# Scans of a three-block kernel on one Trainium2 core: output products regrouped, level runs merged

## The chip, the cores and the metric

One core of one Trainium2 chip runs the whole program. The metric is device time in microseconds (us), the median of several executions. TensorE (PE in the profile) multiplies matrices, its weight loads are PEld; ScalarE is ACT, VectorE is DVE, GpSimd is POOL, and SyncE (SP) issues the DMAs.

## The reference

The input is a sequence of 1024 tokens, 1024 wide. A first block (a delta-rule scan, a convolution, attention to a memory) is followed by two layers of a second one. Each layer has a GLA branch (4 heads, 32 key and 64 value channels), a differential attention branch and an HGRN branch (4 heads, 64 and 64). What matters here is the two-directional gated scan of the GLA and HGRN branches; in the reference it is

```python
def step(state, inp):
    g_n, u_n = inp
    return g_n[..., None] * state + u_n, state
...
o_inter = jnp.einsum('bhntk,bhnkv->bhntv', q * jnp.exp(bcum).astype(q.dtype), s_prev)
return (o_intra + o_inter).reshape(b_, h_, l_, dv).astype(v.dtype)
...
o_f = chunked_gated_scan(q, k_f, v, lg_f)
o_b = flip(chunked_gated_scan(flip(q), flip(k_b), flip(v), flip(lg_b)))
return o_f + o_b
```

So an output of a chunk is a sum of three things: what the forward state of the chunks before gives, what the backward state of the chunks behind gives, and what the tokens of the chunk itself give. Behind it stand a normalisation per head and a gate.

## The kernel before

The kernel keeps channels on the 128 partitions and tokens in the free dimension. The scans of a layer run in `scans` as three scans, i = 0 (GLA, G = 2: four heads of 32 key channels, in two groups g of one head pair each), and i = 1 and 2 (HGRN, G = 1: one head pair of 64 key channels each). A pair has heads e = 0 and 1. Chunks have 64 tokens, n = 0 to 15; j counts pairs of chunks, and x says which chunk of the pair it is, n = 2j + x. `quads` gives the order of cells in which neighbours use different quarters of the array: (x, e) = (0,0), (1,1), (0,1), (1,0).

A scan has three parts. `scan_prep` loads gates and makes decays. `scan_levels` builds the products of tokens within a chunk (AT) over seven levels: for each level and each group, `pairs` makes 32 products of 64 x 64, KK by QQ, into two PSUM banks (`aps`), 16 for the first four j and 16 for the rest, and calls `burst` behind each half. ScalarE (level 0) or VectorE under a mask (levels 1 to 6) takes the two banks into AT. Two banks are all that the pool `a` has. The level's KK comes from a pool of three buffers (tag `kk`), in which the states `S` of both directions lie too. `scan_out` transposes the keys (`KT`), makes the chunk sums (`up`), scans them (`ust`, then `S`, held in `sb[0]` forward and `sb[1]` backward), and writes the output: for each group g and each half hb of the chunks one block into two banks (`ops`). Bank b takes what contracts over partitions HEADS[b]. A block begins with a product with the zero tile `zz` into each bank, which opens all 512 columns (start), and every other product adds. Cell by cell follow a forward state product, a backward state product, both into bank e, and a value product (Vst by AT) into bank x. Then ScalarE copies bank 0 into `os`, VectorE adds bank 1, a burst follows, and `finish_head` of the block before (`last`): Square on ScalarE (`fr<-os`), a product with ones (`fst`), Ln and Exp, then two VectorE operations and the store. There are four blocks a layer for i = 0 and two each for i = 1 and 2, sixteen in all.

A burst is 12 matmuls of 128x512 from a stream of dense projections (`ps`); one call in 14 (SKIP) does nothing. While `pinned` is set, TensorE runs in the order in which the program is written (`mm`, line 250, keeps it). ScalarE, VectorE and SP run in order too, but there a scheduler sets the order when the program is built.

Of the kernel before, what the change touches and what calls it, by code (L numbers as in the profile page):

```python
# [11 lines left out]
BF16 = mybir.dt.bfloat16  # L12
# [134 lines left out]
class Stream:  # L147
# [5 lines left out]
    def burst(self, n=1):  # L153
        while n and (self.g or self.q):
            if self.g is None:
                self.g = self.q.popleft()()
            if self.g is None or next(self.g, True):
                self.g = None
            else:
                n -= 1  # L160
# [18 lines left out]
class Kern:  # L179
# [1290 lines left out]
    def scans(self, l, stream):  # L1470
        nc, tc = self.nc, self.tc
        with ExitStack() as es:
            pool = lambda n, b, **kw: es.enter_context(self.tpool(name="s" + n, bufs=b, **kw))
            p1, p2 = self.s1, self.s2 = pool("1", 1), pool("2", 2)
            self.s3 = pool("3", 3)
            self.fl, self.qt, self.qa, self.qo = (pool("fl", 2, space=PSUM), pool("t", 2, space=PSUM),
                                                 pool("a", 2, space=PSUM), pool("o", 2, space=PSUM))
            self.msk = p1.tile([128, 384], U8, name="msk")
            m = self.staged()[:, 0:384]
            nc.sync.dma_start(out=m, in_=self.A["masks"])  # L1480
            nc.vector.tensor_copy(out=self.msk, in_=m)
            self.zz = p1.tile([1, 128], BF16, name="zz")
            nc.vector.memset(self.zz, 0.0)
            lb = self.lower_bounds(p1) if l else None
            count = iter(range(1000))

            def burst():
                if next(count) % SKIP:
                    stream.burst()
            self.rot = None  # L1490
            left = len(stream.q)
            self.value_rows(stream, l)
            nxt = self.scan_prep(0, l, lb)
            stream.feed(PV)
            self.pinned = True
            for i in range(3):
                cur = nxt
                self.scan_levels(cur, burst)
                if i == 0:
                    stream.reach(left)  # L1500
                if i < 2:
                    nxt = self.scan_prep(i + 1, l, lb)
                else:
                    stream.reach(NEED)
                    qk = self.diff_qk(0, l)
                self.scan_out(cur, l, self.V("hgrn_norm" if i else "gla_norm", l), burst)
            self.pinned = False
            self.head0 = qk, self.diff_v(0, l, self.qt, "t")
            stream.feed(1000)
# [107 lines left out]
    def scan_levels(self, I, burst):  # L1617
# [11 lines left out]
        def pairs(KK, QQ, li):  # L1629
            for g in range(G):  # L1630
                aps = [self.qa.tile([128, 512], F32, tag="a", name="aps") for _ in range(2)]
                for j0 in (0, 4):
                    for j, n, x, e in self.quads(j0, j0 + 4):
                        ns, r = slice(n * 64, n * 64 + 64), cells[2 * g + e][0]
                        self.mm(aps[e][HEADS[x], j * 64:j * 64 + 64], KK[r, ns], QQ[r, ns])
                    burst()
                for e in range(2):
                    dst = AT[g][:, e * 512:e * 512 + 512]
                    if li == 0:
                        self.act(dst, aps[e])  # L1640
                    else:
                        m = self.msk[:, 64 * (li - 1):64 * li].rearrange("p (o c) -> p o c", o=1).to_broadcast([128, 8, 64])
                        nc.vector.copy_predicated(out=c8(dst), mask=m, data=c8(aps[e]))

        KK = T("kk", self.s3)
        self.tt(KK, kf, kb, ALU.add)
# [30 lines left out]
    def scan_out(self, I, l, nw, burst):  # L1677
# [44 lines left out]
        for g in range(G):  # L1722
            for hb in range(2):
                ops = [self.qo.tile([128, 512], F32, tag="o", name="ops") for _ in range(2)]
                for t in ops:
                    self.mm(t, self.zz, self.const[0:1, 0:256].bitcast(BF16), True, False)
                for j, n, x, e in self.quads(4 * hb, 4 * hb + 4):
                    r, h = cells[2 * g + e][0], HEADS[x]
                    o = [t[HEADS[e], n % 8 * 64:n % 8 * 64 + 64] for t in ops]
                    ns, c = slice(n * 64, n * 64 + 64), 512 * e + 64 * j  # L1730
                    last_ = j % 4 == 3 and x != e
                    if n > 0:
                        self.mm(o[e], sb[0][r, n - 1], Q[0][r, ns], False, last_ and n == 15)
                    if n < 15:
                        self.mm(o[e], sb[1][r, 14 - n], Q[1][r, ns], False, last_)
                    self.mm(o[x], Vst[g][h, j, HEADS[e]], AT[g][h, c:c + 64], False, last_)
                o = p2.tile([128, 512], F32, tag="os", name="os")
                self.act(o, ops[0])
                self.tt(o, o, ops[1], ALU.add)
                burst()  # L1740
                last()
                sl = slice(hb * 512, hb * 512 + 512)
# [29 lines left out]
```

## Time and profile before

| | |
|---|---|
| median of 3 runs | 3976.39 us (3974.06 to 3981.07) |
| the profiled execution | 3974.71 us, its span 3972.9 us |
| TensorE busy | 3663.0 us, 92% of the span |
| VectorE, ScalarE, GpSimd busy | 2322.0, 1889.2, 821.7 us |
| mean granted TensorE clock | 0.957 |
| matmul records of the level products (`aps`) | 3584 |
| matmul records of the output products (`ops`) | 960 of states, 512 of values, 32 of zeros |

A float32 matmul leaves two records, one for each of its passes, so 960 records are 480 products. In a timeline a row is a run of equal records: its start, its length to the end of its last record, and how many there were. Records overlap, so the step from one start to the next is what a product costs. The granted clock is a share of 2.4 GHz; the profile knows two levels, 1.2 and 2.4 GHz.

### The profile page before, as it was taken

To read this page: it belongs to the slowest core of one execution; us is meant where nothing else is said; L and a number is where in the kernel's file an instruction comes from. 1 tells how busy PE (TensorE), PEld (TensorE's weight loads), DVE (VectorE), ACT (ScalarE), POOL (GpSimd) and SP (SyncE) were. 2 spreads that over 40 slices of the span, in tenths; PEclk is the share of its full clock that TensorE was granted. 3 is DMA by queue.
4 is the path that set the end of the run, shared out by engine and by line. 5 is a ranking of instruction groups with operands and counts; after the bars stand their busy time and mean duration, and the time that the engine had idled before them with its cause. 6 is when DMAs were issued, how large, how long until landed. Compare 5 with 4: busy or idle time off the path is not lost. (4 is left out here: it accounts for less than half of the span.)

```text
span 3972.9 us, 69665 instructions
## 1 busy us (share of the span) xinstructions
PE 3663.0 (92%) x27554; PEld 2847.4 (72%) x27554; DVE 2322.0 (58%) x4491; ACT 1889.2 (48%) x3429; POOL 821.7 (21%) x710
## 2 busy tenths in 40 slices
PE   7999999999898999989999999999789899998897
PEld 5877666766666677767788667777677667777686
DVE  4246677777767777555544634464883553555863
ACT  4334444444444454444433444454774453545862
POOL 1003323333323333340223200012112100022111
PEclk9999999999999999999999999799999998899998
DMA  4422222222222222347444442222202431223113
GB/s 149 142 88 69 79 79 80 74 77 78 84 79 76 77 85 86 105 154 237 157 154 136 152 141 78 72 84 97 74 33 97 144 111 63 84 94 104 56 35 110
DMA packets 222583, 394.62 MB, mean 99 GB/s; under 512 B 24624, under 2 KB 44080, under 8 KB 222128
## 3 DMA queue, kind: packets, MB, share of 16 engines
q1 hardware_dynamic: 222256, 390.17, 29.5%
q8 instruction: 216, 3.54, 0.4%
q14 instruction: 111, 0.91, 0.1%
HBM read 268.44 MB, written 121.63 MB: 98 GB/s over the span
## 5 line engine op out<-in xcount | busy, mean ns | idle before, releaser
L250 PE MATMUL ps<-hh,whi 128*128 128x512 f32 (+2 forms) x3056 | 1293.2, 423 | 27.6 <-DVE st L202 8.1
L250 PE MATMUL ps<-hl,whi 128*128 128x512 f32 (+2 forms) x3056 | 1207.6, 395 | 4.5 <-DVE hl L202 4.5
L250 PE MATMUL ps<-hh,wlo 128*128 128x512 f32 (+2 forms) x3056 | 1207.3, 396 | 4.7 <-DVE wlo L202 4.6
L250 PEld LDWEIGHTS ps<-hh,whi 128*128 128x128 f32 (+1 forms) x3056 | 585.6, 192 | 199.0 <-issue 31.4
L250 PEld LDWEIGHTS ps<-hh,wlo 128*128 128x128 f32 (+1 forms) x3056 | 585.8, 192 | 138.3 <-DVE wlo L202 6.2
L250 PEld LDWEIGHTS ps<-hl,whi 128*128 128x128 f32 (+1 forms) x3056 | 587.4, 192 | 132.1 <-issue 20.5
L199 ACT ACTIVATE whi<-wraw 128x512 fp32r<-128x512 f32 x486 | 302.6, 625 | 570.0 <-PE ps L250 439.5
L202 DVE TENSOR_TENSOR wlo<-wraw,whi 128x512 fp32r<-128x512 f32 x398 | 294.2, 742 | 417.6 <-ACT whi L199 383.8
L202 POOL TENSOR_TENSOR uacg<-uacg,ut 128x512 f32<-128x512 f32 x240 | 337.6, 1407 | 789.9 <-ACT ut L569 656.1
L202 POOL TENSOR_TENSOR st<-st,rope 128x512 f32<-128x512 f32 x64 | 91.3, 1447 | 978.0 <-DVE st L415 946.5
L199 ACT ACTIVATE st<-ps 128x512 f32<-128x512 f32 (+2 forms) x260 | 149.3, 575 | 264.5 <-PE ps L250 223.9
L573 DVE SCALAR_TENSOR_TENSOR uacc<-uh,vecs,uacc 128x512 f32<-128x512 f32 x224 | 208.3, 930 | 8.0 <-ACT uacc L565 7.1
L202 POOL TENSOR_TENSOR acc<-acc,sq 128x512 f32<-128x512 f32 (+1 forms) x91 | 125.0, 1381 | 294.7 <-ACT sq L199 293.2
L202 POOL TENSOR_TENSOR wlo<-wraw,whi 128x512 fp32r<-128x512 f32 x88 | 121.8, 1385 | 286.7 <-ACT whi L199 259.9
L1387 DVE TENSOR_REDUCE D<-sc 128x1 f32<-128x1024 f32 x128 | 154.7, 1219 | 34.5 <-PE sc L250 33.9
L569 ACT ACTIVATE ut<-uh,vecs 128x512 f32<-128x512 f32 x240 | 166.0, 715 | 4.4 <-POOL uacg L202 3.5
L199 ACT ACTIVATE p<-sc,D 128x1024 f32<-128x1024 f32 x128 | 142.8, 1116 | 41.1 <-DVE D L1387 39.1
L250 PE MATMUL o_ps<-h,wT 128*128 128x128 f32 x1024 | 137.2, 282 | 19.1 <-ACT wT L199 19.1
L250 PEld LDWEIGHTS o_ps<-h,wT 128*128 128x128 f32 x1024 | 131.1, 197 | 27.7 <-ACT wT L199 22.8
L250 PE MATMUL sc<-h,h 128*128 128x512 f32 x256 | 94.0, 448 | 40.7 <-ACT p L199 40.4
L1380 POOL CAST qz<-h 64x128 fp32r<-64x128 f32 x128 | 54.3, 424 | 313.3 <-PE sc L250 304.2
L250 PE MATMUL ps<-oh,wlo 128*128 128x512 f32 x256 | 103.1, 403 | 4.6 <-DVE wlo L202 4.6
(334 smaller groups left out, 6092.8 us busy)
## 6 DMA issues: line engine op xcount, KB each, us to landing
wraw<-in_w_in_dram SPq DMA_DIRECT2D x326, 256.0 KB, 2.8
wraw<-in_w_out_dram SPq DMA_DIRECT2D x76, 256.0 KB, 2.7
g<-st SPq DMA_DIRECT2D x48, 256.0 KB, 2.3
y<-st SPq DMA_DIRECT2D x48, 256.0 KB, 2.0
gt<-y SPq DMA_DIRECT2D x48, 256.0 KB, 2.9
wraw<-in_w_mem_kv_dram SPq DMA_DIRECT2D x32, 256.0 KB, 3.0
yp<-gt SPq DMA_DIRECT2D x32, 256.0 KB, 3.4
yt<-yp SPq DMA_DIRECT2D x32, 256.0 KB, 3.1
```

Source lines behind the costliest of these rows:

```text
L199: self.nc.scalar.activation(out=out, in_=in_, func=func, **kw)
L202: (eng or self.nc.vector).tensor_tensor(out=out, in0=a, in1=b, op=op)
L250: self.pin(self.nc.tensor.matmul(out, lhsT=lhsT, rhs=rhs, start=start, stop=stop))
L569: keep(nc.scalar.activation(out=t, in_=u[:, j:j + 512], func=AF.Copy, scale=w(j)))
L573: keep(nc.vector.scalar_tensor_tensor(out=acc, in0=u[:, k:k + 512], scalar=w(k), in1=acc, op0=ALU.mult, op1=ALU.add))
L1380: nc.gpsimd.tensor_copy(out=Qz[slot][c][HEADS[c]], in_=Qs[c][HEADS[c], ts_])
L1387: nc.vector.reduce_max(out=D[:, c:c + 1], in_=sc, axis=AX.X, negate=True)
```

## The change

The zero tile and its two products per block go. The products of a block are grouped: all forward state products, then all backward ones, then all value products. The first state product into each bank starts it, and the first value product into a bank's other half starts that half. Bank b holds states and values for head b and, in its other half, values alone; so the evacuation is one ScalarE copy of 64 rows per head, and an add of half the columns. In `pairs` the two halves become one run of 32 products, and the two bursts stand behind the evacuation.

```diff
-            self.zz = p1.tile([1, 128], BF16, name="zz")
-            nc.vector.memset(self.zz, 0.0)
...
-                for j0 in (0, 4):
-                    for j, n, x, e in self.quads(j0, j0 + 4):
-                        ns, r = slice(n * 64, n * 64 + 64), cells[2 * g + e][0]
-                        self.mm(aps[e][HEADS[x], j * 64:j * 64 + 64], KK[r, ns], QQ[r, ns])
-                    burst()
+                for j, n, x, e in self.quads():
+                    ns, r = slice(n * 64, n * 64 + 64), cells[2 * g + e][0]
+                    self.mm(aps[e][HEADS[x], j * 64:j * 64 + 64], KK[r, ns], QQ[r, ns])
                 for e in range(2):
...
+                for _ in range(2):
+                    burst()
...
-                for t in ops:
-                    self.mm(t, self.zz, self.const[0:1, 0:256].bitcast(BF16), True, False)
+                part = lambda b, e, n: ops[b][HEADS[e], n % 8 * 64:n % 8 * 64 + 64]
+
+
+                new = [True, True]
+                for d, n0 in ((0, -1), (1, 14)):
+                    for j, n, x, e in self.quads(4 * hb, 4 * hb + 4):
+                        r, sn = cells[2 * g + e][0], n0 - n if d else n + n0
+                        if 0 <= sn < 15:
+                            self.mm(part(e, e, n), sb[d][r, sn], Q[d][r, n * 64:n * 64 + 64], new[e], False)
+                            new[e] = False
                 for j, n, x, e in self.quads(4 * hb, 4 * hb + 4):
-                    r, h = cells[2 * g + e][0], HEADS[x]
-                    o = [t[HEADS[e], n % 8 * 64:n % 8 * 64 + 64] for t in ops]
-                    ns, c = slice(n * 64, n * 64 + 64), 512 * e + 64 * j
-                    last_ = j % 4 == 3 and x != e
-                    if n > 0:
-                        self.mm(o[e], sb[0][r, n - 1], Q[0][r, ns], False, last_ and n == 15)
-                    if n < 15:
-                        self.mm(o[e], sb[1][r, 14 - n], Q[1][r, ns], False, last_)
-                    self.mm(o[x], Vst[g][h, j, HEADS[e]], AT[g][h, c:c + 64], False, last_)
+                    h, c = HEADS[x], 512 * e + 64 * j
+                    self.mm(part(x, e, n), Vst[g][h, j, HEADS[e]], AT[g][h, c:c + 64], x != e and j % 4 == 0, j % 4 == 3)
                 o = p2.tile([128, 512], F32, tag="os", name="os")
-                self.act(o, ops[0])
-                self.tt(o, o, ops[1], ALU.add)
+                two = lambda t, e, x: t[HEADS[e]].rearrange("p (j x c) -> p j x c", x=2, c=64)[:, :, x]
+                for e in range(2):
+                    self.act(o[HEADS[e]], ops[e][HEADS[e]])
+                    self.tt(two(o, e, 1 - e), two(o, e, 1 - e), two(ops[1 - e], e, 1 - e), ALU.add)
                 burst()
```

On TensorE, at the first output block of the first layer's scan i = 0 (h are the decayed queries, S the states, AT the products within a chunk, Vst the values), before:

```order
L250 LDWEIGHTS zz
L250 MATMUL ops<-const,zz 128x512
L250 LDWEIGHTS zz
L250 MATMUL ops<-const,zz 128x512
L250 MATMUL ops<-h_22196,S 64x64
L250 MATMUL ops<-AT_22356,Vst 64x64
L250 MATMUL ops<-h_22194,S 64x64
L250 MATMUL ops<-h_22196,S 64x64
L250 MATMUL ops<-AT_22356,Vst 64x64
```

and now the whole block, to the first dense product behind it:

```order
L250 MATMUL ops<-h_22192,S 64x64 x14
L250 MATMUL ops<-h_22194,S 64x64 x16
L250 MATMUL ops<-AT_22354,Vst 64x64 x16
L250 MATMUL ps<-hh_94,whi 128x512
```

State and value products no longer alternate: 30 of the one form stand ahead of 16 of the other, the forward states' first.

On ScalarE, at the end of the same scan (kk are the copies for the next scan's levels and h of 128x256x2 its queries, e and h of 128x1024 the gates of the scan after that; st and whi belong to the dense stream, os and fr to the output), before:

```order
L199 ACTIVATE kk<-h_23403 128x512
L199 ACTIVATE kk<-h_23404 128x512
L199 ACTIVATE kk<-h_23403 128x256x2
L199 ACTIVATE os<-ops 128x512
L199 ACTIVATE kk<-h_23404 128x256x2
L199 ACTIVATE whi<-wraw 128x512
L199 ACTIVATE fr<-os 128x512
L199 ACTIVATE fr<-fst,const 128x512
```

and now, of the 25 rows from the first kk to the last block's fr<-os, the last twelve:

```order
L199 ACTIVATE whi<-wraw 128x512
L199 ACTIVATE st<-ps 128x512
L199 ACTIVATE h_24267<-h_23399 128x256x2
L199 ACTIVATE os<-ops 64x512
L199 ACTIVATE st<-st 128x512
L199 ACTIVATE h_24724<-h_24724 128x1024
L199 ACTIVATE st<-st,const 128x512
L199 ACTIVATE os<-ops 64x512
L199 ACTIVATE h_24720<-h_24720 128x1024
L199 ACTIVATE e<-h_24722 128x1024
L199 ACTIVATE st<-st 128x512
L199 ACTIVATE fr<-os 128x512
```

The last block's evacuation and Square moved behind the next levels' copies and behind half of the gates of the scan after it.

## Rows read from the trace of the kernel before

**Rows 1.** The page, part 1: busy time, share of the span, instructions.

```profile
PE 3663.0 (92%) x27554; PEld 2847.4 (72%) x27554; DVE 2322.0 (58%) x4491; ACT 1889.2 (48%) x3429; POOL 821.7 (21%) x710
```

**Rows 2.** Stretches of the scans: length, busy us of each engine, granted clock, DMA.

```profile
2349.15:2446.34 97.19, 95.28 (x1210) 72.63 (x1210) 45.78 (x75) 42.50 (x66) 0.00 (x0) 1.00 0.23 80
...
2472.93:2532.39 59.46, 59.46 (x323) 43.59 (x323) 7.56 (x11) 11.68 (x20) 0.00 (x0) 0.63 0.11 36
2532.39:2580.06 47.67, 44.00 (x376) 32.48 (x375) 32.88 (x51) 33.88 (x54) 0.00 (x0) 0.82 0.34 117
3339.08:3397.06 57.98, 57.98 (x323) 42.53 (x323) 7.55 (x11) 11.69 (x20) 0.00 (x0) 0.65 0.11 37
3397.06:3445.79 48.73, 43.82 (x376) 32.23 (x375) 34.75 (x54) 33.93 (x54) 0.00 (x0) 0.83 0.34 114
2633.11:2652.26 19.15, 17.99 (x230) 13.79 (x229) 11.58 (x18) 8.08 (x15) 2.92 (x3) 1.00 0.26 84
2729.27:2742.78 13.51, 13.31 (x214) 10.96 (x214) 5.21 (x10) 5.21 (x9) 5.29 (x4) 1.00 0.22 74
...
2652.26:2703.17 50.91, 48.08 (x605) 36.67 (x605) 33.38 (x62) 20.83 (x37) 11.04 (x8) 1.00 0.29 95
```

**Rows 3.** TensorE's timeline in the levels of scan i = 0: start, length, run.

```profile
2349.15 1.16 PE L250 MATMUL aps<-h,kk 32*64 32x64 f32 x64
2350.24 0.50 PE L250 MATMUL ps<-h,hh 128*128 128x512 f32 x1
...
2432.10 0.69 PE L250 MATMUL aps<-h,kk 32*64 32x64 f32 x32
2432.72 0.50 PE L250 MATMUL ps<-hh,whi 128*128 128x512 f32 x1
...
2435.36 0.39 PE L250 MATMUL ps<-hh,wlo 128*128 128x512 f32 x1
2435.68 0.69 PE L250 MATMUL aps<-h,kk 32*64 32x64 f32 x32
```

**Rows 4.** TensorE's timeline in the first output block of scan i = 0.

```profile
2472.93 0.60 PE L250 MATMUL ops<-const,zz 1*128 1x512 bf16 x2
2473.46 0.32 PE L250 MATMUL ops<-h,S 32*64 32x64 f32 x2
...
2473.97 0.44 PE L250 MATMUL ops<-h,S 32*64 32x64 f32 x4
...
2482.33 0.68 PE L250 MATMUL ops<-h,S 32*64 32x64 f32 x4
...
2483.34 0.68 PE L250 MATMUL ops<-h,S 32*64 32x64 f32 x4
...
2488.41 0.63 PE L250 MATMUL ps<-hh,wlo 128*128 128x512 f32 x1
2488.84 0.63 PE L250 MATMUL ps<-hh,whi 128*128 128x512 f32 x1
```

**Rows 5.** TensorE's timeline behind the fourth output block of scan i = 0.

```profile
2554.88 1.02 PE L250 MATMUL fst<-fr,const 128*128 128x512 f32 x2
2555.83 0.69 PE L250 MATMUL aps<-h,kk 64*64 64x64 f32 x32
```

**Rows 6.** Groups of ScalarE, shapes kept apart: a copy of 64 rows.

```profile
L199 ACT ACTIVATE h<-st 64x512 fp32r<-64x512 f32 x96 | 60.3, 628 | 4.8 <-DMA st<-d1k 2.1 <-PE sc L250 0.7 <-DMA st<-d0k 0.2
```

**Rows 7.** ScalarE's timeline at the fourth output block of scan i = 0.

```profile
2544.50 1.23 ACT L199 ACTIVATE kk<-h 128x512 f32<-128x512 f32 x2 [9.04 <-PE ops L250]
...
2551.23 0.61 ACT L199 ACTIVATE fr<-os 128x512 f32<-128x512 f32 x1
...
2554.52 1.06 ACT L199 ACTIVATE e<-h 128x1024 f32<-128x1024 f32 x1
```

**Rows 8.** The level banks' tile aps: what idle engines waited for (us, times).

```profile
  DVE AT L1643: 17.2, 39
```

**Rows 9.** TensorE's timeline: the chunk sums of scan i = 0.

```profile
2450.07 1.89 PE L250 MATMUL up<-Vst,KT 64*32 64x64 f32 x128
```

## The prediction

> **What bounds the kernel now.** The page comes first: TensorE is busy for 92% of the span [rows 1], so time must come out of its stream, or out of its clock. Next comes the table of stretches, for the two layers' scans, where alone the diff acts. In the levels of the first head pairs (GLA, i = 0) TensorE is busy 95.28 of 97.19 us at the full clock, 2.4 GHz. The output blocks behind them are also wholly busy, but the granted clock there is 0.63 and 0.65, most of the time the lower level of 1.2 GHz: these stretches (59.46 and 57.98 us) hold only three of the four blocks and three dense bursts [rows 2]. The timeline of TensorE shows why they are long, and the order of the built programs shows what each queue stands behind.
>
> In the levels, 64 product records start within 1.09 us and 32 within 0.62 us [rows 3] (each float32 product leaves two records). Thirty-two more cost 0.47 us, 14.6 ns a record, with four 64x64 corners of the array at work in turn; a run has 0.15 us of its own. One corner alone takes a record every 58 to 60 ns: two more state records lengthen a GLA group from 0.32 to 0.44 us [rows 4]. The GLA output alternates state products of 32 rows with value products of 64 rows, so each group of six records takes 1.01 us (2482.33 to 2483.34), 168 ns a record, at the low clock, where a dense product takes 0.43 us [rows 4] in place of 0.23 [rows 3]. The HGRN output, with all products at 64 rows, needs nothing like that: both its blocks, a burst of twelve and a second burst fit in 13.51 us at clock 1.00 [rows 2].
>
> **The change, part by part**, on the profiled execution: 3974.7 us, 1.7 under the median shown; its span is 3972.9.
>
> **1. GLA output blocks.** Per block stand 60 state records and 32 value records. Grouped, the state records use two corners alternately: 29 ns each by the four-corner row, 1.76 us. The value records use four: 0.47. With 0.15 for the start and 0.15 for the single change of shape, a block takes 2.5 us. Both zero products go with it (0.53 us a pair: 2472.93 to the first product at 2473.46 [rows 4]). No row shows two corners alternating, so bounds: 14.6 ns (0.88 us) to 58 ns (3.5 us) for the state part; I take the middle, since the records of two corners overlap already in the HGRN block, where a block of 92 records takes 3.8 us with its zero products (13.51 less two bursts, halved [rows 2]), not the 5.3 that 58 ns each would make. With small work this short the clock should hold, as it does around the HGRN blocks. A burst is 12 x 0.23 plus 0.21 of changing over: 2.95 us (2432.72 to 2435.68 [rows 3]); a head normalisation's product takes 0.95 (2554.88 to 2555.83 [rows 5]). From the first block to the start of the fourth: 3 x 2.5 + 3 x 2.95 + 2 x 0.95 = 18.25 us in place of 59.46 and 57.98: **minus 40.5 us a layer.** The evacuation is now two ScalarE copies of 64 rows and two half-width VectorE adds. A 64-row copy is as long as one of 128 rows, 0.63 us [rows 6], so 0.6 us more ScalarE work a block; the 2.95 us burst hides it. If that cover were gone, 0.6 x 16 = 10 us.
>
> **2. The fourth GLA block and the next scan's first three levels.** These take 47.67 and 48.73 us [rows 2], with ScalarE busy 33.9 and VectorE 33 to 35: nearly as much as TensorE needs. Now the queues matter. The level copies kk wait for the buffers of the states (ScalarE's idle of 9.04 us at 2544.50 [rows 7]). Grouping frees the forward states after a third of the fourth block, so the scheduler puts kk copies and the next gates' preparation (e, h) ahead of the last evacuation on ScalarE: 23 rows now stand between the first kk and the Square (fr<-os), where five did. With that kk, six are 1024 wide at about 1.08 us, 18 some 0.62 us [rows 7]: 17.7 us; waits for VectorE's multiplications between the kk copies add about 8, worked out from 0.65 us per 512-wide and 1.2 per 1024-wide multiplication. So that Square ends some 27 us after the block's start, and TensorE, in order, stands before the last normalisation product (fst) from 9.4 us on: **about 17 us idle, at a clock that then falls.** Behind it: fst 0.95, then three levels of 1.09 + 5.7 us, one short of a burst of 2.95. The third is over at 27.5 + 0.95 + 17.4 = 46, and 2 to 3 us more for products at the low clock: 49 in place of 48. **Plus 1 a layer.** TensorE alone would need 28 us (the blocks and bursts above): the lower end, minus 20; the upper, both engines wholly in series (33.9 + 32.9 = 67), plus 19.
>
> **3. Levels.** One run of 64 records and two bursts take 1.09 + 24 x 0.2285 + 0.21 = 6.78 us; two runs of 32 and their bursts took 7.16 [rows 3]. GLA has 14 pairs of runs and 26 bursts a layer: 14 x 1.30 + 26 x 2.74 = 89.5 in place of 97.19 [rows 2]; I take 7 us, leaving 0.7 for waits. The waits for the masked copies, 17.2 us in all [rows 8], fall with it, as 5.7 us of dense work instead of 2.95 stand before the banks are needed again. The last scan: 7 x 1.30 + 13 x 2.74 = 44.8 in place of 50.91: minus 6. The four remaining levels of the middle scan: minus 1.4.
>
> **4. HGRN output.** Last scan: 2 x 2.4 + 2.95 + 2.87 = 10.6 in place of 13.51, minus 2.9. Middle scan: 19.15 us today. There too the kk copies and their multiplications move ahead of the evacuation. The chain from the freed forward states to the Square (12 ScalarE rows alternating with 11 of VectorE, half of them in series) comes to 14 us, and fst lands 5 us later than today: plus 5.
>
> **Sum.** Minus 40.5 plus 1 minus 7 minus 6 minus 1.4 minus 2.9 plus 5 = minus 51.8 a layer, minus 104 for two: 3871 in this execution, **3873 us** against the median. Pools, DMAs and SP's queue keep their work; a transfer has more burst time per level run than before. The zz tile's removal (one memset a layer) is nothing.
>
> **Rivals.**
> *No blockage.* If ScalarE and VectorE get through their rows sooner than my chain, TensorE alone sets steps 2 and 4: minus 20 and minus 8 a layer more, 3817 in full, 3845 at half. For it: kk may start earlier than I count. Against it: these rows stand in the queue whatever their speed. 24%.
> *The state products don't overlap* (the change does not do what its grouping says): 60 x 58 ns, 1.74 us a block more, 16 blocks: 28 us, 3901. For it: in the GLA block nothing overlaps today. 10%.
> *The clock still falls in the GLA output.* Then a burst takes 4.9 us and a block 4: 3.4 x 3 blocks x 2 layers = 20, 3893. Against it: small-tile work per block is no denser in HGRN, at clock 1.00 [rows 2]. 10%.
> *Evacuation binds.* ScalarE (two copies, Square, Ln, Exp, and the burst's own rows: 5 us) and VectorE (3.5 us) in series would make a block and burst 8.5 us instead of 6.1, and step 2 67 us: 2 x (3 x 2.4 + 18) = 50 more, 3923. 6%.
> The Trainium skill's page TensorEngine Tiling (Performance Considerations, PSUM Bottleneck) warns of this: "After 4× TensorE speedup, PSUM copy may become bottleneck". By that rule this case would be the likely one; today's rows show the evacuation waiting for the products instead, so no run here bears it out yet.
> *Slower than before.* The merged runs let the clock fall in the levels. Forty-six bursts a layer lie there; at 0.43 instead of 0.23 us a product they cost 46 x 12 x 0.2 = 110 us a layer, 220 in all. From 47% of the level bursts at the low clock on, the 104 us are lost; at 60%, 4005. Against it: runs of 64 records (2349.15 [rows 3]) and of 128 (2450.07, 1.8 us [rows 9]) stand in today's stretches at clock 1.00. 3%.
>
> **How the numbers follow.** The forecast has 47%. A measurement of this kernel tells about 0.2%, 8 us, from no change; every case but the last is well beyond it: faster 96%, slower 3%, same 1%. The range, 3832 to 3905, takes in the two rivals near 3900 and the half of *no blockage* up to its middle, and leaves out its far half (12%), evacuation and slower (9%).
>
> **What would show it.** Right: in the GLA output stretches state records in one run of 1.6 to 1.9 us and value records in 0.5; clock near 1.00 up to the fourth block; no zz; a run of aps of 64 records in 1.09 us, then 24 dense products; a TensorE idle of 10 to 20 us before the last fst of the GLA scans, released by ScalarE's fr; fewer waits on AT. Wrong: state records 58 ns apart; the low clock from the first GLA block on; no idle before that fst (then the time is nearer 3830); idle at every block for os (then evacuation binds).

## The result, and the profile after

The changed kernel takes 3860.18 us (median of 4 runs, 3856.55 to 3863.20), the kernel before 3976.06 in the same comparison: ratio 0.9706, 95% interval 0.9690 to 0.9723, so 2.8 to 3.1% faster. The forecast was 3873, within 3832 to 3905. The profiled execution took 3856.55 us (span 3854.7), against 3974.71 before.

The page, part 1, answers to [rows 1]; TensorE is busy for 131.6 us less, the others for hardly more.

```profile
PE 3531.4 (92%) x27522; PEld 2766.1 (72%) x27522; DVE 2330.0 (60%) x4505; ACT 1898.7 (49%) x3445; POOL 824.4 (21%) x710
```

The stretches of the scans answer to [rows 2], in the same columns: length, busy us of PE, PEld, DVE, ACT and POOL, granted clock, DMA share, GB/s. In order: the GLA levels; the GLA output to the start of its fourth block; the fourth block and the next scan's first three levels; the middle scan's output; the last scan's levels and its output; then the second layer's GLA output stretches.

```profile
2341.94:2437.84 95.90, 92.28 (x1210) 73.53 (x1210) 46.23 (x75) 42.29 (x66) 0.00 (x0) 0.96 0.23 79
2464.81:2484.50 19.69, 18.50 (x318) 14.62 (x317) 7.42 (x14) 11.91 (x21) 0.00 (x0) 1.00 0.35 109
2484.50:2525.37 40.87, 30.19 (x372) 22.96 (x373) 34.30 (x56) 36.71 (x57) 0.00 (x0) 0.87 0.39 130
2576.98:2596.22 19.24, 15.74 (x226) 12.06 (x225) 14.48 (x25) 10.98 (x19) 2.73 (x3) 1.00 0.29 98
2596.22:2641.09 44.87, 44.87 (x605) 36.17 (x605) 33.04 (x57) 18.92 (x34) 11.07 (x8) 1.00 0.29 96
2667.75:2680.10 12.35, 10.95 (x210) 9.30 (x209) 4.50 (x10) 5.83 (x10) 5.36 (x4) 1.00 0.20 66
3267.34:3286.84 19.50, 18.50 (x317) 14.61 (x316) 7.42 (x14) 11.92 (x21) 0.00 (x0) 1.00 0.34 111
3286.84:3328.23 41.39, 29.57 (x372) 22.44 (x372) 37.16 (x60) 36.24 (x57) 0.00 (x0) 0.88 0.39 128
```

The GLA output went from 59.46 and 57.98 us to 19.69 and 19.50, and the clock there from 0.63 and 0.65 to 1.00. That is where the time came from. The third and the last row are new in kind: TensorE is busy for only 30 of 41 us, ScalarE for 36 to 37.

TensorE's timeline (start, length, instruction, count, idle before it and its releaser) shows three places: a wait within a merged burst of the levels, the first GLA block, and the last normalisation product of the GLA scan.

```profile
2374.31 0.50 PE L250 MATMUL ps<-hh,whi 128*128 128x512 f32 x1
...
2380.95 0.80 PE L250 MATMUL ps<-hh,whi 128*128 128x512 f32 x1 [3.62 <-DVE st L202]
2381.54 0.63 PE L250 MATMUL ps<-hl,whi 128*128 128x512 f32 x1
2381.97 0.63 PE L250 MATMUL ps<-hh,wlo 128*128 128x512 f32 x1
...
2464.81 1.96 PE L250 MATMUL ops<-h,S 32*64 32x64 f32 x60
2466.70 0.69 PE L250 MATMUL ops<-AT,Vst 64*64 64x64 f32 x32
2467.33 0.50 PE L250 MATMUL ps<-hh,whi 128*128 128x512 f32 x1
...
2504.69 2.07 PE L250 MATMUL fst<-fr,const 128*128 128x512 f32 x2 [10.54 <-ACT fr L199]
2506.70 1.99 PE L250 MATMUL aps<-h,kk 64*64 64x64 f32 x64
```

A block takes 2.52 us (2464.81 to 2467.33), where [rows 4] had 1.01 us for every six of its 92 records. Before fst, TensorE stands idle for 10.54 us (11.68 in the second layer), and fst and the level products behind it then run at half pace. The wait at 2380.95 was not foreseen: the merged run of 24 dense products takes 12.00 us (2374.31 to 2386.31; 13.16 in the second layer) in place of 5.7, the last twelve of them 0.43 us apart, the low clock's pace.

All of TensorE's waits from 2340 to 2700 us (what for, us in total, times, longest):

```profile
PE fst L250 <- ACT fr L199: 11.9, 2, 10.5
PE ps L250 <- DVE st L202: 5.2, 2, 3.6
PE up L250 <- ACT KT L199: 2.7, 4, 1.1
PE ops L250 <- ACT os L199: 2.5, 2, 1.3
PE ops L250 <- DVE os L202: 2.2, 1, 2.2
```

ScalarE's timeline answers to [rows 7]: from the first kk copy to the Square of the fourth block.

```profile
2487.33 1.22 ACT L199 ACTIVATE kk<-h 128x512 f32<-128x512 f32 x2
...
2490.40 1.06 ACT L199 ACTIVATE e<-h 128x1024 f32<-128x1024 f32 x1 [0.22 <-DMA h<-s2z]
...
2497.79 0.59 ACT L199 ACTIVATE os<-ops 64x512 f32<-64x512 f32 x1
...
2500.48 0.59 ACT L199 ACTIVATE os<-ops 64x512 f32<-64x512 f32 x1
2501.60 1.06 ACT L199 ACTIVATE h<-h 128x1024 f32<-128x1024 f32 x1 [0.53 <-DVE h L208]
...
2504.03 0.61 ACT L199 ACTIVATE fr<-os 128x512 f32<-128x512 f32 x1
```

Of all rows from that kk to the Square only two have idle time of over 0.1 us ahead of them, 0.22 and 0.53 us: the Square is late because ScalarE is working. It does wait earlier, before the third block's evacuation, for the store (d_y) of the first block; os has two buffers:

```profile
2482.78 0.59 ACT L199 ACTIVATE os<-ops 64x512 f32<-64x512 f32 x1 [3.90 <-DMA d_y<-os]
```

### The profile page after: what moved, and what is told of

Its sections match the earlier page's. It is cut to its first block, busy times and chain, and to the rows that moved or that the text cites. A ratio compares the mean times of both kernels' runs of the same rounds, so it can differ in the third digit from the quotient of the medians.

```text
span 3854.7 us, 69637 instructions
## 1 busy us (share of the span) xinstructions
PE 3531.4 (92%) x27522; PEld 2766.1 (72%) x27522; DVE 2330.0 (60%) x4505; ACT 1898.7 (49%) x3445; POOL 824.4 (21%) x710
```

## The experiments

Times are medians; the change itself is at 3860, ratio 0.9706. "Scans" below is, for each layer, from the first level product to the end of the last output block in the profiled run: 390.8 and 390.8 us before, 335.4 and 337.3 after. Each short diff is against the changed kernel unless it says otherwise.

### Each half of the change alone

Grouping alone, the level runs as before:

```diff
-                for j, n, x, e in self.quads():
...
+                for j0 in (0, 4):
+                    for j, n, x, e in self.quads(j0, j0 + 4):
...
+                    burst()
...
-                for _ in range(2):
-                    burst()
```

> The changed kernel with the level runs in two halves again, a burst behind each half. Theory (two parts that act apart: grouping takes about 46 us a layer out of the GLA outputs and the stretch behind them, merging some 10 us a layer out of the levels): the GLA output up to the fourth block stays at 19 to 20 us, clock 1.00; the last scan's levels go back to 51 us; the stall for ps<-st in the GLA levels, which stands between the two bursts of a merged run, goes. Time 3860 + 2 x (6 + 2 + 1) = 3878 (3872 to 3890). Rival A (grouping alone carries it, merged runs only trade a wait for another): 3860, within 6. Rival B (the bursts moved behind the evacuation are what keeps the clock up in the GLA output): the low clock comes back there, 3920 or more.

Measured: 3882.87 us, ratio 0.9761 (0.9742 to 0.9781). The GLA output is at 19.65 us, clock 1.00; the first layer's GLA levels take 100.05 us up to the first chunk sum (99.63 in the change by that measure), with four waits of 1.0 us together; scans 349.4 and 349.7.

Merging alone, against the kernel before:

```diff
-                for j0 in (0, 4):
-                    for j, n, x, e in self.quads(j0, j0 + 4):
...
+                for j, n, x, e in self.quads():
...
+                for _ in range(2):
+                    burst()
```

> The kernel before with the level runs merged and the two bursts behind them, output products as before. Theory: the GLA output stays at 59 us and clock 0.63, the last scan's levels fall from 51 to 45 us, the GLA levels from 97 to between 90 and 96; 2 x (6 + 1.4 + 1.3 to 7) = 17 to 29 us less than before: 3947 to 3959. Together with the run that only groups, the two differences from before add to that of the whole change (116 us) within 8. Rival A (merging does nothing): 3976. Rival B (merging is what brought the clock back): the GLA output below 45 us, time under 3910.

Measured: 3964.04 us, ratio 0.9973 (0.9958 to 0.9988), above the 3947 to 3959 expected. The GLA output is still at 59.58 us, clock 0.63. Scans 387.5 and 388.5. The last scan gained 5 us up to its output's start, but a run of 24 dense products in the second scan's levels waits 5.69 us for st and takes 14.1 us, so that most of the rest is lost.

What follows: grouping brings 93 of the 116 us by itself, merging 11 to 12; their sum is 104 of 116, which was expected within 8 and missed. In the whole times these 12 us are hardly clear of noise, as each ratio is known to about 0.2%, 8 us; in the scans of the profiled runs, one of each kernel, the two do not add (82.5 and 5.6 against 108.9). Rival B of both runs falls: neither where the bursts stand nor the merged runs touch the clock in the GLA output.

### The order alone

Zero products gone, half evacuations and merged levels kept, but the products cell by cell:

```diff
-                for d, n0 in ((0, -1), (1, 14)):
-                    for j, n, x, e in self.quads(4 * hb, 4 * hb + 4):
+                for j, n, x, e in self.quads(4 * hb, 4 * hb + 4):
+                    for d, n0 in ((0, -1), (1, 14)):
...
-                for j, n, x, e in self.quads(4 * hb, 4 * hb + 4):
                     h, c = HEADS[x], 512 * e + 64 * j
...
```

> The changed kernel without zero products and with its half evacuations and merged levels, but forward state, backward state and value product cell by cell, as before. Theory (the alternation of 32-row and 64-row products is what costs 168 ns a record and the clock): the GLA stretch up to the fourth block is back at 55 to 59 us with a granted clock of 0.6 to 0.7, the HGRN blocks stay as in the changed kernel; time 3860 + 2 x 38 + 2 x 5 for the fourth block = 3946 (3930 to 3955). Rival A (the zero products, which write 512 columns of both banks, and the whole-bank add cost it): 3860 to 3875. Rival B (the alternation costs the changes of shape, about 0.15 us each and 30 a block, but not the clock): blocks of 7 us at clock 1.00, 3860 + 8 x 4.5 = 3896.

Measured: 3975.07 us, ratio 0.9996 (0.9983 to 1.0010): the whole gain is gone. Two stretches within its first block, the whole to the fourth block and the first block of the next (HGRN) scan, and then TensorE's timeline in the first block:

```profile
2468.00:2469.00 1.00, 1.00 (x12) 0.80 (x10) 0.35 (x1) 1.00 (x2) 0.00 (x0) 1.00 0.00 0
...
2472.50:2476.00 3.50, 3.50 (x23) 2.78 (x22) 0.00 (x0) 0.00 (x0) 0.00 (x0) 0.50 0.03 9
...
2466.86:2522.06 55.20, 55.20 (x317) 41.27 (x316) 8.01 (x14) 13.12 (x22) 0.00 (x0) 0.66 0.12 39
...
2627.95:2631.07 3.12, 3.12 (x93) 3.06 (x92) 2.86 (x4) 1.45 (x3) 0.23 (x1) 1.00 0.22 84
```

```profile
2468.50 0.44 PE L250 MATMUL ops<-h,S 32*64 32x64 f32 x4
2468.87 0.32 PE L250 MATMUL ops<-AT,Vst 64*64 64x64 f32 x2
2469.12 0.44 PE L250 MATMUL ops<-h,S 32*64 32x64 f32 x4
...
2471.51 0.68 PE L250 MATMUL ops<-h,S 32*64 32x64 f32 x4
...
2472.52 0.68 PE L250 MATMUL ops<-h,S 32*64 32x64 f32 x4
```

The block begins at the full clock, and a cell of six records then costs 0.62 us (2468.50 to 2469.12); with the clock at 0.50 it costs 1.01 (2471.51 to 2472.52). Grouped, it costs 2.52 / 16 = 0.16. So the gain has two parts, by an estimate from these rows. At 0.62 us a cell, three blocks would cost 3 x (16 x 0.62 - 2.52) = 22 us more than grouped ones at the full clock throughout; of the other 18 of the 40 us a layer, 1.6 are three pairs of zero products and some 16 the low clock, in the blocks and in the bursts behind them.

The HGRN block tells the change of form from the order of cells. All its products are 64 rows, so the same order has no change of form there. It takes 3.12 us, against 2.36 in the change, and stays at clock 1.00: the order alone costs 0.05 us a cell, of the 0.46 that a GLA cell pays.

The time is above the 3930 to 3955 expected. The next stretch is 13.4 us longer where 5 were allowed (105.90 us to the start of the second scan's output against 92.48, with a wait of 6.88 us before fst), and the HGRN blocks did not stay as they were.

### How much grouping is enough

The same products grouped within each pair of chunks, and within two cells (the second kernel differs from the first in the cells of a group):

```diff
+                for jj in range(4 * hb, 4 * hb + 4):
+                    for d, n0 in ((0, -1), (1, 14)):
+                        for j, n, x, e in self.quads(jj, jj + 1):
...
+                for c2 in (quads[m:m + 2] for m in range(0, len(quads), 2)):
+                    for d, n0 in ((0, -1), (1, 14)):
+                        for j, n, x, e in c2:
```

> The changed kernel with the products of an output block grouped by form within each pair of chunks only: forward states, backward states, values, then the next pair. A GLA block has 8 runs of two forms instead of 2, where the alternating order had some 30. Theory (each change of form costs, and dense alternation costs the clock besides): 7 more changes of 0.15 us and less overlap, a GLA block of 3.6 to 4.5 us; if the clock stays, 3860 + 8 x 1.5 = 3872 (3868 to 3880); if it falls, bursts of 4.4 to 5.3 us and blocks of 5 to 8, 3895 to 3915. Rival A (only strict cell by cell order costs; runs of two to four are as good as one long run): 3860, blocks 2.5 us. Rival B (any return to the 32-row form within a block costs as before): 3960 or more.

Measured: 3866.58 us, ratio 0.9725 (0.9708 to 0.9743), which the whole times cannot tell from the change; the blocks can, 3.42 us against 2.52.

> The changed kernel with the output products grouped by form within two cells: two to four state products, two value products, and so on, 16 runs of one form in a GLA block where the changed kernel has 2, the grouping by pair of chunks 8 and the alternating order 32. Theory (0.15 us for a change of form at the full clock, worked out from the blocks of 2.52 and 3.42 us with 1 and 7 changes): 15 changes, a block of 4.6 us; if the clock stays 3860 + 8 x 2.1 = 3877 (3872 to 3882). If the clock falls as in the alternating order (31 changes, 7.0 us by the same price, measured 12.3 to 14.3 us at the low clock): blocks of 8 to 9 us, bursts of 4.4 us and more, 3905 to 3935. Rival (the price of a change is not constant, the alternating order pays for neighbours in one corner instead): a block below 4 us, 3868 or less.

Measured: 3877.88 us, ratio 0.9762 (0.9743 to 0.9781). That is the time expected for a clock that stays, but the clock fell, and the stretch to the fourth block is 12.1 us longer than in the change, where three blocks at the expected 2.1 us more make 6.3: the agreement is luck. Stretches of the kernel grouped by pair (to the fourth block, and the first block), then of the one grouped by two cells (first block, the burst behind it, second block, and all to the fourth):

```profile
2471.08:2491.96 20.88, 20.88 (x318) 15.94 (x317) 7.60 (x14) 12.15 (x21) 0.00 (x0) 1.00 0.33 102
2471.08:2474.50 3.42, 3.42 (x93) 2.88 (x93) 1.50 (x3) 2.87 (x5) 0.00 (x0) 1.00 0.00 0
```

```profile
2466.96:2473.12 6.16, 6.16 (x93) 4.78 (x92) 1.98 (x3) 2.85 (x5) 0.00 (x0) 0.77 0.26 85
2473.12:2477.93 4.81, 4.81 (x15) 3.52 (x13) 0.84 (x2) 1.95 (x4) 0.00 (x0) 0.58 0.01 3
2477.93:2483.02 5.09, 5.09 (x94) 4.01 (x93) 2.07 (x3) 3.07 (x5) 0.00 (x0) 1.00 0.18 52
2466.96:2498.75 31.79, 31.79 (x318) 23.62 (x317) 8.00 (x14) 12.91 (x22) 0.00 (x0) 0.79 0.23 67
```

The price of a change of form comes out of the two timelines, at the full clock.

```profile
2471.84 0.68 PE L250 MATMUL ops<-h,S 32*64 32x64 f32 x16
2472.45 0.34 PE L250 MATMUL ops<-AT,Vst 64*64 64x64 f32 x8
2472.73 0.68 PE L250 MATMUL ops<-h,S 32*64 32x64 f32 x16
```

```profile
2477.93 0.45 PE L250 MATMUL ops<-h,S 32*64 32x64 f32 x8
2478.30 0.33 PE L250 MATMUL ops<-AT,Vst 64*64 64x64 f32 x4
2478.56 0.45 PE L250 MATMUL ops<-h,S 32*64 32x64 f32 x8
```

A group of four cells takes 0.89 us (2471.84 to 2472.73), one of two 0.63: two cells cost 0.26, and the remaining 0.37 belong to the group's two changes, 0.18 us each. Sixteen cells at 0.13 and two changes are then 2.45 us, against the 2.52 measured for a whole block. The alternating order pays more than this sum (0.13 + 0.37 = 0.50, measured 0.62). Both state products of a cell lie in one corner of the array there, and 0.05 of the 0.12 is what the HGRN block pays for that order; the rest is not explained. With 31 changes in a block the clock falls in every block, with 15 in the first and third of the four, with 7, or with 1 as in the change, in none. The Trainium skill says why a change of form may cost: "Changing tiling mode (not just tile) drains the TensorE" (TensorEngine Tiling (Array Packing), Tiling Modes, Key Properties). These rows agree that such a change costs time, 0.18 us here; that the engine drains no run shows.

### Corners

State products of head 0 first, then of head 1:

```diff
-                    for j, n, x, e in self.quads(4 * hb, 4 * hb + 4):
+                    for j, n, x, e in sorted(self.quads(4 * hb, 4 * hb + 4), key=lambda c: c[3]):
```

> The changed kernel with the state products of a block ordered head 0 first, then head 1, so that neighbours lie in one corner of the array. Theory (the state products of two corners overlap, 29 ns a record for two, 58 for one): a GLA block grows from 2.5 to 4.2 us, the time by 1.7 x 16 = 28 us less what waits hide in the fourth blocks: 3880 to 3888. Rival A (their pace is the issue of the queue, not the corners): no block grows, 3860. Rival B (the slower run of small products takes the clock down): over 3900.

Measured: 3876.10 us, ratio 0.9738 (0.9713 to 0.9762), below the 3880 to 3888 expected; scans 344.3 and 348.2.

```profile
2474.13 3.17 PE L250 MATMUL ops<-h,S 32*64 32x64 f32 x60
2477.23 0.69 PE L250 MATMUL ops<-AT,Vst 64*64 64x64 f32 x32
2477.86 0.75 PE L250 MATMUL ps<-hh,whi 128*128 128x512 f32 x1
```

Sixty state records take 3.10 us, 52 ns each, against 1.89 us and 31.5 ns with two corners in turn. The corners overlap; the price of one alone, 58 ns, was 6 ns too high, so the block grew by 1.2 us and not 1.7. The clock is 1.00 in the first block and 0.93 over this GLA stretch: it fell in the burst behind the first block, which took 4.54 us.

### The zero products

```diff
+                for t in ops:
+                    self.mm(t, self.zz, self.const[0:1, 0:256].bitcast(BF16), True, False)
...
```

> The changed kernel with the two products with the zero tile ahead of each block again, all others adding. Theory (a plain cost, 0.53 us a block): blocks of 3.0 instead of 2.5 us, 3860 + 16 x 0.53 = 3868, less what the waits of the fourth blocks hide: 3865 to 3869. Rival A (the zero products, which write both banks whole, wait for the evacuation of the bank's other half or take the clock down): 3880 or more. Rival B (hidden): 3860.

Measured: 3861.89 us, ratio 0.9717 (0.9687 to 0.9747). Blocks of 3.05 us, 0.53 more, and scans of 339.3 and 341.2 us, some 4 more each, as the theory has it (8 x 0.53 = 4.2); the runs scatter by 27 us, so the whole time cannot tell this from nothing.

### The wait before the last normalisation

Three buffers for the evacuated block, the second with ScalarE's order also held as written:

```diff
...
-                o = p2.tile([128, 512], F32, tag="os", name="os")
+                o = p2.tile([128, 512], F32, tag="os", name="os", bufs=3)
```

> The changed kernel with three instead of two buffers for the evacuated output block os (room for it from small vectors of the first block of the program, which are given back behind that block). In the built program the fourth GLA block's evacuation and Square then stand 6 rows earlier on ScalarE: 17 rows lie between the first kk and fr<-os instead of 23. Theory (the idle before the last fst of the GLA scans is the place of fr<-os in ScalarE's queue): about 6 rows of 0.6 to 1 us less, idle 5 to 7 us instead of 10.5 and 11.7, time 3850 (3846 to 3856). Rival A (the wait is for the buffer, that is for the store of the second block): idle below 2 us, 3840. Rival B (the two engines' work in that stretch binds, 36.7 and 34.3 of 40.9 us): the idle moves behind fst, before the level products, 3860.

Measured: 3845.58 us, ratio 0.9674 (0.9654 to 0.9694), the lowest median of this study. Its interval just overlaps that of the change (0.9690 to 0.9723), but all four of its runs (3842.83 to 3849.87) lie below all four of the change. Scans 329.9 and 333.9, so 5.5 and 3.4 us less. The idle before fst is 4.93 us in the first layer and 3.7 in the second, at and below the theory's 5 to 7. Rival A was right at another place: the third block's evacuation no longer waits for the first block's store (3.90 us in the change, 3.70 in its second layer), and the stretch to the fourth block, 19.69 us in the change, is

```profile
2468.03:2486.47 18.44, 18.44 (x317) 14.61 (x317) 7.83 (x14) 13.12 (x22) 0.00 (x0) 1.00 0.37 112
```

The second kernel's further edit (the copies of os, the kk copies of two levels and the gates' first rows in the same way):

```diff
+    def kept(self, out, in_, func=AF.Copy, **kw):
...
+            self.tc.keep_in_program_order(self.nc.scalar.activation(out=out, in_=in_, func=func, **kw))
...
-        self.act(r, o, AF.Square)
+        self.kept(r, o, AF.Square)
...
```

> Three buffers for os, and ScalarE's order kept as the program is written for the copies of os, the Squares, the kk copies of the next scan's levels 1 and 2, and the first row of each gate: the last evacuation and Square now stand ahead of the gates of the scan after the next. Theory (queue order): the idle before the last fst of the GLA scans falls below 2 us, the stretch from the fourth block to the fourth level run from 40.9 to 31 us, 3860 - 2 x 9 = 3842 (3836 to 3850). Rival A (the engines' work binds, or the second level's copies, which now come later, do): the idle reappears before the level products, 3856 to 3866. Rival B (delayed gates come too late for the HGRN scans): the last scan's levels wait, over 3866.

Measured: 3883.53 us, ratio 0.9765 (0.9748 to 0.9783), slower than the change, as Rival B had it (over 3866). Holding that much in written order made new waits on TensorE; the two largest of those from 2340 to 2620 us:

```profile
PE fst L254 <- ACT fr L203: 11.3, 3, 6.0
PE ps L254 <- DVE st L206: 3.8, 1, 3.8
```

Its GLA levels, though, to the first chunk sum again, are what was forecast of merging: no wait stands in them, and ScalarE has 39.28 us to do beside them, not 44.34 as in the change (44.53 with grouping alone):

```profile
2342.78:2436.09 93.31, 93.31 (x1229) 74.92 (x1228) 45.38 (x76) 39.28 (x66) 0.00 (x0) 1.00 0.26 88
```

Two lighter ways followed. The first has three buffers, and only the gates of the scan after the next and the second level's copies are issued later: the copies and the first gate behind the last Square, the second gate behind a later level's copies. The second way also holds the two gates of the next scan in the GLA levels, each behind the copies of a level (its expectation names the second gate alone). `behind` issues what it holds behind the instruction so marked; the diff is the second way's, and in the first way the entries (1, 0) and (1, 1) hold nothing.

```diff
+            with self.behind({(1, 0): (0, 2), (1, 1): (0, 4), (2, 0): "sq", (2, 1): (1, 2)}.get((i, d))):
+                e = self.ln1p(z)
...
+            with self.behind("sq" if li == 1 and I["i"] else None):
+                self.act(vw(KK)[:, :, 0], vw(kf)[:, :, 0])
...
```

> As the run with three os buffers, and on ScalarE the gates of the scan after the next and the next scan's kk copies for level 2 are issued behind the Square of the last block: 9 rows instead of 17 lie between the first kk and fr<-os; nothing else is held back. Theory (ScalarE's queue order sets the idle before the last fst): the idle of 4.9 us in the GLA scans falls below 2 us, and the second scan's wait with it; 3846 - 2 x 4 = 3838 (3833 to 3842). Rival (the stretch is bound by the two engines' work, so that it comes back before the level products): 3843 to 3848, level runs behind it late.

Measured: 3847.53 us, ratio 0.9680 (0.9664 to 0.9696): the rival's time and not the theory's. The wait before fst is down to 2.1 us, and another stands behind it:

```profile
PE ps L254 <- DVE st L206: 6.5, 1, 6.5
PE fst L254 <- ACT fr L199: 2.1, 1, 2.1
```

> As the run before it, and the second gate of the next scan is issued behind the fourth level's copies of the GLA levels instead of wherever the scheduler put it, so that the two gates no longer stand together in ScalarE's queue. Theory (the wait ps<-st within a merged run of 24 dense products, 5 to 7 us a layer with the low clock behind it, comes from the two gates' 1024-wide rows ahead of the dense stream's evacuation): runs of 24 all at 5.7 us, GLA levels 93 to 94 us, 3838 - 2 x 6 = 3826 (3821 to 3832). Rival A (the work only moves: the wait comes back behind a later level): 3834 to 3840. Rival B (merging the GLA levels saves nothing even without that wait): the levels stay at 98 to 101 us with no idle seen.

Measured: 3849.32 us, ratio 0.9690 (0.9671 to 0.9708), above the ranges of the theory and of Rival A. GLA levels of 97.00 and 97.81 us instead of 100.12 and 100.89; the long run of 24 is still 9.17 and 10.09 us.

Last, three buffers and the gates of the GLA levels alone:

```diff
+            with self.behind({(1, 0): (0, 2), (1, 1): (0, 4), (2, 0): None, (2, 1): None}.get((i, d))):
+                e = self.ln1p(z)
```

> Three os buffers, the scheduler's own order at the outputs, and only the second gate of the next scan held behind the fourth level's copies in the GLA levels. Theory (the wait inside a merged run can be made smaller there, 9.2 and 10.1 us a run instead of 11 to 13, without touching the outputs' stretch, where the three buffers alone did best): the GLA levels 97 us instead of 98.5 and 100.7, the rest as with three buffers: 3846 - 4 = 3842 (3838 to 3846). Rival (ScalarE's and VectorE's work is one sum over levels and outputs, so whatever is moved out of one comes back in the other): 3846 to 3850.

Measured: 3847.39 us, ratio 0.9685 (0.9671 to 0.9698), the rival's time and not faster than three buffers alone. In the first layer the scans fell to 328.1 us; in the second (335.2) the time came back behind the outputs, where the stretch of the table below takes 93.84 us against 88.94 with three buffers alone.

What follows is seen in one stretch, from the start of the fourth GLA block to the start of the second scan's output in the first layer (length, busy us and granted clock from the stretches of each profile):

| kernel | length | PE | DVE | ACT | clock |
|---|---|---|---|---|---|
| before | 100.72 | 96.56 | 63.77 | 62.59 | 0.92 |
| merging alone | 101.18 | 94.05 | 63.82 | 63.58 | 0.92 |
| grouping alone | 98.41 | 85.03 | 64.59 | 65.12 | 0.93 |
| the change | 92.48 | 81.32 | 64.64 | 65.88 | 0.94 |
| three buffers, order held as written | 96.26 | 84.79 | 64.97 | 63.07 | 0.93 |
| three buffers, gates behind the Square | 92.19 | 83.05 | 63.88 | 63.35 | 0.94 |
| the same, and GLA gates held | 92.21 | 83.05 | 63.89 | 63.41 | 0.94 |
| three buffers, GLA gates held | 88.60 | 81.52 | 64.10 | 64.01 | 0.96 |
| three buffers | 88.50 | 81.37 | 64.08 | 63.99 | 0.98 |

ScalarE's and VectorE's work is nearly the same in all. Over half of it lies in the stretch's first 40 us (36.71 of 40.87 us on ScalarE in the change), where TensorE needs 28 by the prediction's estimate. Reordering moved the idle from fst to the dense stream's bank and gave nothing; the third buffer gave 4 us here. Why it gains what the order does not isn't settled. In the change ScalarE idles for less than 0.1 us ahead of the fourth block's evacuation (2497.79), so the store of the second block holds it back for no more than that; with the third buffer the scheduler also put the evacuation six rows earlier, and no run gives it the buffer and the old place in the queue.

## Why the prediction was right, and where not

By its own steps, us a layer on the profiled runs:

| step | predicted | first layer | second layer |
|---|---|---|---|
| 1. GLA output to the fourth block | -40.5 | -39.8 | -38.5 |
| 2. fourth block, next three levels | +1 | -6.8 | -7.3 |
| 3. GLA levels | -7 | -1.3 | -0.1 |
| 3. last scan's levels | -6 | -6.0 | -5.3, to its output's start |
| 3. rest of the middle scan's levels | -1.4 | -1.4 | -1.6 |
| 4. middle HGRN output | +5 | +0.1 | +0.1 |
| 4. last HGRN output | -2.9 | -1.2 | -1.1 |

The scans as a whole gained 55.4 and 53.5 us, 108.9 together, where the steps gave 103.6; stretches that the steps leave out, between levels and outputs, lost some 1 us a layer. The profiled runs differ by 118.2; 7.2 of the rest lie ahead of the first scan, where nothing is changed and where the profiles of this study scatter from 2341.94 to 2351.00 us.

**Step 1 was right in mechanism and size.** A block was to take 2.5 us and takes 2.52; a burst 2.95; the clock holds. The stretch is 19.69 instead of 18.25, as the fourth block starts 1.19 us late for the third block's evacuation. That one waits for the first block's store, which "the 2.95 us burst hides it" left out; with three buffers the stretch is 18.44. The middle value for two corners (29 ns a record) measured 31.5. That grouping is the cause, and not the zero products, the evacuation or the level runs, is shown by the alternating run, which differs from the change in the order of the output products alone. Why the clock falls with it stays open. The rivals *the state products don't overlap* and *the clock still falls in the GLA output* are excluded by this step's rows.

**Step 2 named the right wait, with a wrong size.** TensorE does stand before the last fst behind ScalarE's queue, 10.5 and 11.7 us, not 17. The failed term is "waits for VectorE's multiplications between the kk copies add about 8": ScalarE goes from the first kk (2487.33) to the end of the Square (2504.64) in 17.3 us, just the 17.7 of its rows' durations, with 0.75 us of idle. The scheduler had put independent rows into those gaps, and a chain of waits was added to work that covers it. The +5 of step 4 came from the same kind of chain: the middle scan's fst waits 1.3 us, its second block 2.2 us for os where it waited 1.2 before, the blocks are shorter by about as much, and the stretch is as long as it was.

**Step 3 missed a wait.** Merging is worth 7 us in the GLA levels (93.31 us where no wait stands in them, 100.05 unmerged), but in the changed kernel TensorE then runs ahead of ScalarE and VectorE while these work on the next scan's 1024-wide gates, and a dense run waits for its bank: 6.3 us in the first layer with the low clock behind it, 7.5 in the second. "Leaving 0.7 for waits" was the term that failed. The waits for the masked copies, as [rows 8] counts them, did fall, from 17.2 to 0.7 us. The errors of the steps (8 and 5 us too dear in 2 and 4, 6 and 2 too cheap in 3 and 4) largely cancel. That the sum, 3873, came within 13 us of the 3860 measured is to that extent luck; step 1 is not.

**Step 4, last output:** the second block waits 1.27 us for the first one's os, which the sum left out.

**The rivals.** *No blockage* was the nearest: of the 28 us a layer that it takes off steps 2 and 4, some 13 came; the time is not at its half, 3845, mainly because step 3 gave some 6 us a layer less. *Evacuation binds* did not come true: in the first three GLA blocks TensorE is busy for 18.50 of 19.69 us, and the stretch of step 2 takes 40.87 us and not 67. What holds TensorE there is ScalarE's whole queue (36.71 us), not the copies, 0.59 us each. The Trainium skill's warning on PSUM copies (TensorEngine Tiling (Array Packing), Performance Considerations, PSUM Bottleneck) is borne out only to a small extent: late evacuations held TensorE for 4.7 us of the first layer's scans (the two ops rows of the list of waits). *Slower* fell: the levels' clock is 0.96 and 1.00.

## What to carry to other kernels

Where small products of two shapes feed one accumulation, order them by shape: here a change cost 0.18 us at the full clock, and a stream of such changes took the clock down for the dense work behind it as well. When TensorE's part of a stretch shrinks, compare its new length with the other engines' busy time there; if theirs is near, an idle that is moved by reordering may come back a few microseconds later, as it did here (10.5 us before fst became 2.1 there and 6.5 at the dense stream's bank), and the gain of the next edit in that stretch is not to be counted in full. When blocks get shorter, look also at the buffers that they are evacuated into: here two were too few, since a store had to land first. A chain of waits should be added to an in-order queue's work only for rows that have no independent ones to fill the gaps.

## What was not expected of the hardware

TensorE can be busy for 100% of a stretch and still be granted half its clock: in the alternating block it is busy for 3.50 of 3.50 us at 0.50. How often the form changes matters, but isn't all: with groups of two cells the clock fell in the first block (0.77) and the burst behind it (0.58) and was back at 1.00 for the second; with the state products in one corner and a single change it fell too, to 0.93 over the stretch. What decides it, no run here shows. After a wait of 3.62 us within a burst the next twelve dense products ran at the lower level, 0.43 us each, so that wait cost 6.3 us.
